# Earlier scaling for the wide score blocks of a gated linear recurrence, and one more weight step in front of them

## The chip, the cores and the metric

The kernel runs on one core of one Trainium2 chip. The metric is the device time of one execution in microseconds (us), as a median over runs; lower is better. The engines are called PE (TensorE matmul), PEld (its weight loads), DVE (VectorE), ACT (ScalarE), POOL (GpSimd) and SP (SyncE, which issues most transfers).

## The reference

One layer of a hybrid decoder on 1024 positions of width 1024, in float32. Two token mixers run beside each other, an RG-LRU and an HGRN2 recurrence with 8 heads of width 128; their outputs are merged by sigmoid gates, projected and added to the input. An MLP with a squared ReLU follows. The change lies in the HGRN2 part:

```python
def step(state, chunk):
    qc, kc, lfc, vc = chunk
    cum = jnp.cumsum(lfc, axis=2)
    o_inter = jnp.einsum('bhtk,bhkv->bhtv', qc * jnp.exp(cum), state)
    rel = cum[:, :, :, None, :] - cum[:, :, None, :, :]
    decay = jnp.where(causal[:, :, None], jnp.exp(jnp.minimum(rel, 0.0)), 0.0)
    scores = jnp.einsum('bhtsk,bhsk->bhts', qc[:, :, :, None, :] * decay, kc)
    o_intra = jnp.einsum('bhts,bhsv->bhtv', scores, vc)
    ...
    state = jnp.exp(last)[..., None] * state + jnp.einsum('bhsk,bhsv->bhkv', k_to_end, vc)
    return state, o_inter + o_intra
```

The kernel never takes logarithms: it multiplies keys and queries by products of forget gates over blocks of growing width (2, 8, 32, 64, 128 positions), so that each block of scores is a plain matrix product.

## The kernel before, in words

The sequence is worked in two parts of 512 positions (`c` = 0, 1), and in each part the heads go in four pairs (`p` = 0 to 3). So the code around the change runs eight times, once for each (c, p); these are called the eight pairs below, the first four with c = 0. After each part comes the output projection, and at the end the MLP, which the change doesn't touch.

A pair projects v, xa, q and f, then starts `hgrn`. While `hgrn` builds its operands on DVE, PE works on the projections g, mb, ga and ma of the same pair. They are a generator, `rest`, of 32 steps; a step is six products of 128x512 (`mm3` three times two, L123 to L125), and eight steps make one projection. `go(n)` runs n steps. The list `GO` says how many run before each part of `hgrn`: 17 steps before the narrow score blocks, GO[1] before the wide ones, then one before the transposes of the keys, one before the products that make the states, two before the output products, and the rest at the end. All products inside a pair are pinned: PE keeps the order in which the code issues them. DVE and ACT take the order that a scheduler gave them at build time.

The steps that matter, with the lines of the profile:

- narrow score blocks, L420: `pt1`, `pt2` (level 2) and `pt8` (level 8), 32 products of 128x48 each; DVE copies them under masks into `dd` (L410 and L431 for the own block, L439 six times for the levels), and POOL copies `dd` into `scT` (L515)
- scaling on DVE (`mul`, L410): first `kc` in place, then `qb` in place twice, then `kk` from `kc` and `qf` from `qb`; ACT copies the other halves of `kk` and `qf` (L528, L529)
- wide score blocks: 16 products from `kc` and `qb` (L538, block of 32) and 8 from `kk` and `qf` (L549, block of 64); ACT copies both into `scT` (L554, L555)
- `kk` and `qf` scaled once more by halves (L410), transposes of `kk` (`pk`, L576), ACT copies `kT` (L580), products `pkv` (L585), states `sn` on DVE (L594, L596), output products `po` (L610, L613), ACT squares and copies (L617, L623), the scaled output `on` on DVE (L410), transposes `poT` (L655)
- between these, weights of later projections are split into two parts: a cast on ACT (`wH`, L78) and a subtraction on DVE (`wL`, L79)

PSUM has eight banks under three tags: `pj` with four for the projections, `sc` and `hg` with two each, taken in turn. Before the change `pt1`, `pt2` and both wide blocks are under `sc`; `pt8`, `pk`, `pkv`, `po` and `poT` are under `hg`.

Of the kernel before, what the change touches and what calls it, by code (L numbers as in the profile page):

```python
# [18 lines left out]
P = 128  # L19
# [12 lines left out]
OUT_TILES = 8  # L32
QUADS = 16
LEVELS = (2, 8)
GO = (17, 4, 1, 1, 2)
OWN_BEFORE = 2


# [5 lines left out]
def trunk(ctx: ExitStack, tc: tile.TileContext, x, wts, mlp, pv, gains, mask_f, mask_u, out):  # L44
    nc = tc.nc
    V, A, G, PE = nc.vector, nc.scalar, nc.gpsimd, nc.tensor
# [13 lines left out]
    def bank(tag, name):  # L60
        return ps.tile([P, 512], F32, tag=tag, name=name, bufs={"pj": 4, "sc": 2, "hg": 2}[tag])
# [116 lines left out]
    def mt(tag, name, shape=(P, T), dt=F32, bufs=1):  # L178
        return m.tile(list(shape), dt, tag=tag, name=name, bufs=bufs)
# [111 lines left out]
    def run(steps, n=None):  # L291
        while n is None or n > 0:
            try:
                next(steps)
            except StopIteration as end:
                return end.value
            if n is not None:
                n -= 1
# [95 lines left out]
    def f_of(c, p, pp):  # L394
        ff = mt("f", f"f{c}{p}", (P, 2 * T))
        kk = mt("kk", f"kk{c}{p}", (P, 2 * T))
        for s in range(2):
            u = 2 * p + s
            f, k = ff[:, s * T : (s + 1) * T], kk[:, s * T : (s + 1) * T]
            A.activation(f, pp[s], AF.Sigmoid)  # L400
            A.activation(k, pp[s], AF.Sigmoid, scale=-1.0)
            V.tensor_scalar(f, f, omlb[:, u : u + 1], lb[:, u : u + 1], op0=ALU.mult, op1=ALU.add)
            V.tensor_scalar(k, k, omlb[:, u : u + 1], None, op0=ALU.mult)
        V.tensor_scalar(ff, ff, F_MIN, 1.0, op0=ALU.max, op1=ALU.min)
        return ff, kk

    def hgrn(c, p, q1, f, kk, v, go, scan):

        nm = f"{c}{p}"
        mul = lambda o, a, b: V.tensor_tensor(out=o, in0=a, in1=b, op=ALU.mult)  # L410
        dd = mt("dd", f"dd{nm}", (P, 8, 32))

        def blocks(k_, rhs, name, tag="sc"):

            pt = bank(tag, f"sc{name}_{nm}")[:, : 8 * 48].rearrange("p (n t) -> p n t", n=8)
            for n in range(8):
                for b in range(4):
                    k = 4 * n + b
                    pin(
                        PE.matmul(  # L420
                            pt[32 * b : 32 * b + 32, n, :], k_[:, 32 * k : 32 * k + 32], rhs(k), start=True, stop=True
                        )
                    )
            return pt

        def own_block(pt):
            pt = pt.rearrange("p n (a b) -> p n a b", b=3)
            d2 = dd.rearrange("p n (a b) -> p n a b", b=2)
            mf2 = mf.rearrange("p (a b) -> p a b", b=2).unsqueeze(1)
            mul(d2, pt[:, :, :, 0:2], mf2.to_broadcast([P, 8, 16, 2]))  # L430
            V.copy_predicated(dd[:, :, 1::2], mu[:, 0, :, 1::2], pt[:, :, :, 2])  # L431

        def level_blocks(li, cw, pt):
            pt = pt.rearrange("p n (a x) -> p (n a) x", x=6 * cw)
            dg = dd.rearrange("p n (a x) -> p (n a) x", x=4 * cw)
            for d, a in ((1, 0), (2, 3), (3, 5)):
                w = (4 - d) * cw
                m_ = mu[:, 3 * li + d, :, :].rearrange("p n (a x) -> p (n a) x", x=4 * cw)
                V.copy_predicated(dg[:, :, d * cw :], m_[:, :, d * cw :], pt[:, :, a * cw : a * cw + w])  # L439
# [4 lines left out]
        qa = mt("qa", f"qa{nm}", (P, 1792)).rearrange("p (a b c) -> p a b c", b=7, c=2)  # L444
# [13 lines left out]
        def take(n):  # L458
            nonlocal off
            off += n  # L460
            return seg[:, off - n : off]

        def sums(t4, g):
            after = take(3 * g).rearrange("p (a b) -> p a b", b=3)
            before = take(2 * g).rearrange("p (a b) -> p a b", b=2)
            mul(before[:, :, 0], t4[:, :, 0], t4[:, :, 1])
            mul(after[:, :, 1], t4[:, :, 2], t4[:, :, 3])
            G.tensor_scalar(after[:, :, 2], t4[:, :, 3], 1.0, 0.0, op0=ALU.mult, op1=ALU.add)  # L468
            mul(before[:, :, 1], before[:, :, 0], t4[:, :, 2])
            mul(after[:, :, 0], t4[:, :, 1], after[:, :, 1])  # L470
            return before, after

        def level_q(q4, t4, g, cw):
            mul(q4[:, :, 5, :], q4[:, :, 3, :], t4[:, :, 2:3].to_broadcast([P, g, cw]))
            mul(q4[:, :, 4:7:2, :], q4[:, :, 2:6:3, :], t4[:, :, 1:2].unsqueeze(3).to_broadcast([P, g, 2, cw]))

        c0, c1 = LEVELS
# [4 lines left out]
        kc = mt("kc", f"kc{nm}", (P, 2 * T))  # L482
# [14 lines left out]
        level_q(q4, t4, g1, c1)  # L497
        go(GO[0] - (OWN_BEFORE if c > 0 else 0))
        pt1 = blocks(kk, lambda k: q1[:, 16 * k : 16 * k + 16, :], "1")
        if c > 0:  # L500
            go(OWN_BEFORE)
        pt2 = blocks(kb, lambda k: qa[:, k * g0 // 32 : (k + 1) * g0 // 32, 1:7, :], str(c0))
        pt8 = blocks(kc, lambda k: q4[:, k * g1 // 32 : (k + 1) * g1 // 32, 1:7, :], str(c1), "hg")
        before, after = sums(t4, g1)
        own_block(pt1)
        level_blocks(0, c0, pt2)
        level_blocks(1, c1, pt8)
        mul(k4(kc, c1)[:, :, 0:3, :], k4(kc, c1)[:, :, 0:3, :], after.unsqueeze(3).to_broadcast([P, g1, 3, c1]))
        mul(q4[:, :, 1, :], q4[:, :, 1, :], t4[:, :, 0:1].to_broadcast([P, g1, c1]))
        mul(q4[:, :, 2:4, :], q4[:, :, 2:4, :], before.unsqueeze(3).to_broadcast([P, g1, 2, c1]))  # L510
        tc_ = take(g1)
        mul(tc_, before[:, :, 0], after[:, :, 1])
        qv = qb[:, :, 0:32]
        for b in range(4):
            G.tensor_scalar(  # L515
                scT[32 * b : 32 * b + 32, :, 32 * b : 32 * b + 32],
                dd[32 * b : 32 * b + 32, :, :],
                1.0,
                0.0,
                op0=ALU.mult,  # L520
                op1=ALU.add,
            )

        q8 = qv.rearrange("p (a e) c -> p a e c", e=2)
        pairs = lambda k: k.rearrange("p (a e c) -> p a e c", e=2, c=32)
        t8 = tc_.rearrange("p (a e) -> p a e", e=2)
        qf = mt("qa", f"qf{nm}", (P, 1792))[:, 0:1024]
        A.copy(pairs(kk)[:, :, 1, :], pairs(kc)[:, :, 1, :])  # L528
        A.copy(pairs(qf)[:, :, 0, :], q8[:, :, 0, :])  # L529
        mul(pairs(kk)[:, :, 0, :], pairs(kc)[:, :, 0, :], t8[:, :, 1:2].to_broadcast([P, 16, 32]))  # L530
        mul(pairs(qf)[:, :, 1, :], q8[:, :, 1, :], t8[:, :, 0:1].to_broadcast([P, 16, 32]))
        go(GO[1])
        pt = bank("sc", f"sc32_{nm}")[:, :256].rearrange("p (n t) -> p n t", n=8)
        for n in range(8):
            for b in (0, 2):
                k = 4 * n + b
# [34 lines left out]
        vn = lambda s, n: v[:, n, s * P : (s + 1) * P]  # L571
        go(GO[2])
        pk = [bank("hg", f"pk{c}{u}") for _, u in both]
# [4 lines left out]
        for s, u in both:  # L578
            kT.append(mt(("kT", "rr")[s], f"kT{c}{u}", (P, 4, P)))
            A.copy(kT[s][:, :nkv, :], pk[s][:, : nkv * P].rearrange("p (n k) -> p n k", n=nkv))  # L580
        go(GO[3])
        pkv = [bank("hg", f"pkv{c}{u}") for _, u in both]
# [5 lines left out]
        for s, u in both:  # L588
            sn = sn2[:, s]
            states.append([scar[:, u, :]] + [sn[:, n, :] for n in range(4)])  # L590
            for n in range(nkv):
# [3 lines left out]
                else:  # L595
# [7 lines left out]
                    )  # L603
        go(GO[4])
        po = [bank("hg", f"po{c}{u}") for _, u in both]
# [89 lines left out]
    for c in range(NC):  # L695
# [6 lines left out]
        for p in range(NPAIR):  # L702
            v = project_v(c, f"{c}{p}")
            px = project(c, f"xa{c}{p}")
            if c == 0 and p == 0:
                parameters()
                tc.keep_in_program_order(V.tensor_copy(mu, mu32.to_broadcast([P, 7, 8, 32])))
            xc3 = conv(c, p, px)
            pinned[0] = True
            q1 = q_of(c, p, project(c, f"q{c}{p}"))  # L710
            steps = project_steps(c, f"f{c}{p}")
            run(steps, 2)
            got = {}
            with tc.high_priority(300):
                rg = rg_lru(c, p, *xc3)
            f, kk = f_of(c, p, run(steps))
            rest = gates(c, p, got, ys)


            def scan():  # L720
                got["h"] = rg_scan(c, p, *rg)

            got["on"] = hgrn(c, p, q1, f, kk, v, lambda n: run(rest, n), scan)
            run(rest)
            pinned[0] = False
# [209 lines left out]
    for q in range(QUADS):  # L935
        n = q + 1 if q + 1 < QUADS else QUADS + QUADS - 2
# [79 lines left out]
    for kb in range(n_kb):  # L1016
        last = kb + 1 == n_kb
        qs = order[2 * kb : 2 * kb + 2]
        for half in range(2):
            pairs = (2 * half, 2 * half + 1)  # L1020
# [110 lines left out]
```

## Time and profile before

| | |
|---|---|
| median of 3 runs | 1605.46 us (1605.14, 1605.46, 1609.54) |
| profiled execution, its own time | 1608.64 us |
| its span, first to last instruction | 1606.8 us |
| busy share of PE, DVE, ACT | 97%, 75%, 47% |
| mean granted clock of PE | 0.995 of full |

Rows of the timeline have the start in us from the span's start, the duration in us, the engine, the line, the operation and its tiles, how many were merged into the row (`x32` for 16 products counts their weight loads too), and in brackets the idle time of the engine just before, with what ended it. Rows of the waits name who waited, for whom, and then the total in us, the number of times and the longest. Products overlap in PE, so their durations add up to more than the time that passes; the difference of two starts is the better measure.

### The profile page before, as it was taken

What the parts mean: (1) busy time and instruction counts of PE and PEld (TensorE: products, weight loads), DVE (VectorE), ACT (ScalarE), POOL (GpSimd) and SP (SyncE); (2) the same over time, 40 slices, a digit from 0 to 9 for tenths busy, and PEclk for the clock granted to TensorE, in tenths of its full rate; (3) what the DMA queues carried; (4) which work ended last, traced back from release to release, by engine and by line L of the source; (5) the groups of instructions that cost most, each with busy time, mean ns of one, the idle gap of its engine ahead of it and who ended that gap; (6) DMA issues with size and microseconds to landing.
All of it is one profiled execution on the core that took longest, in us unless ns stands there. A gap on an engine that the chain in (4) does not pass through costs nothing.

```text
span 1606.8 us, 23139 instructions
## 1 busy us (share of the span) xinstructions
PE 1562.4 (97%) x9240; PEld 1306.6 (81%) x9240; DVE 1200.3 (75%) x1703; ACT 748.8 (47%) x1186; POOL 92.7 (6%) x107
## 2 busy tenths in 40 slices
PE   7999999999999999999999997999999999999998
PEld 6888888788788888798888875888888878888886
DVE  5885865848853774956858788888888888888876
ACT  4643445345333544445435465766777731222113
POOL 0020010200200110100100100000000000000000
PEclk9999999999999999999999998999999999999999
DMA  6212212222243222222222362666666675666652
GB/s 239 93 66 92 93 66 101 83 80 92 80 168 134 92 79 80 93 79 96 76 92 92 120 209 103 251 239 253 254 236 249 233 266 227 254 251 255 257 206 105
DMA packets 57996, 246.51 MB, mean 153 GB/s; under 512 B 6688, under 2 KB 6816, under 8 KB 47136
## 3 DMA queue, kind: packets, MB, share of 16 engines
q1 hardware_dynamic: 56304, 239.27, 39.8%
q10 hardware_dynamic: 1584, 5.77, 1.0%
q8 instruction: 72, 1.18, 0.3%
q14 instruction: 36, 0.29, 0.1%
HBM read 185.24 MB, written 59.77 MB: 152 GB/s over the span
## 4 chain that ended last, share of the span: by engine, by line
PE 78%; DVE 15%; issue 2%; ACT 2%; DMA 1%; POOL 1%; DVEq 0%; POOLq 0%; ACTq 0%; SPq 0%
PE dX L123 3%; PE dX L124 3%; PE dX L125 3%; PE uX L123 3%; PE uX L125 3%; PE uX L124 3%; DVE wL L79 2%; PE pj_ma L125 2%; PE pj_ma L123 2%; PE pj_xa L123 2%; PE pj_xa L124 2%; PE pj_ma L124 2%; PE pv L123 2%; PE pv L124 2%; PE pj_f L123 2%
## 5 line engine op out<-in xcount | busy, mean ns | idle before, releaser
L79 DVE TENSOR_TENSOR wL<-raw,wH 128x1024 fp32r<-128x1024 f32 x160 | 195.4, 1221 | 132.3 <-ACT wH L78 130.6
L78 ACT CAST wH<-raw 128x1024 fp32r<-128x1024 f32 x160 | 167.6, 1047 | 131.9 <-PE po L124 27.3
L1043 DVE TENSOR_TENSOR acc<-acc,dX 128x512 f32<-128x512 f32 x128 | 85.0, 683 | 29.4 <-PE dX L125 29.0
L78 ACT CAST wA<-q 128x512 fp32r<-128x512 f32 x32 | 19.8, 622 | 132.6 <-PE dX L125 101.4
L468 POOL TENSOR_SCALAR seg<-seg 128x128 f32<-128x128 f32 (+1 forms) x16 | 31.6, 1974 | 443.9 <-DVE seg L410 443.9
L1043 DVE TENSOR_TENSOR acc<-acc,dY 128x512 f32<-128x512 f32 x64 | 43.5, 685 | 15.6 <-PE dY L125 14.5
L369 DVE RECIPROCAL rr<-rr 128x512 f32<-128x512 f32 x16 | 53.5, 3341 | 0.0
L903 ACT ACTIVATE b<-b 128x512 f32<-128x512 f32 x48 | 30.2, 630 | 37.4 <-DVE b L902 37.4
L364 DVE TENSOR_SCALAR rw<-rw 128x1024 f32<-128x1024 f32 x8 | 5.5, 694 | 43.7 <-ACT rw L360 43.7
L123 PE MATMUL pv<-wH,hT0H 128*128 128x256 f32 x128 | 37.2, 291 | 0.0
L124 PE MATMUL pv<-wL,hT0H 128*128 128x256 f32 x128 | 36.9, 288 | 0.0
L125 PE MATMUL pv<-wH,hT0L 128*128 128x256 f32 x128 | 36.8, 288 | 0.0
L123 PE MATMUL pv<-wH,hT1H 128*128 128x256 f32 x128 | 36.5, 285 | 0.0
L124 PE MATMUL pv<-wL,hT1H 128*128 128x256 f32 x128 | 36.2, 283 | 0.0
L125 PE MATMUL pv<-wH,hT1L 128*128 128x256 f32 x128 | 36.2, 283 | 0.0
L332 DVE SCALAR_TENSOR_TENSOR xc<-xp,pvt,xc 128x512 f32<-128x512 f32 x48 | 33.1, 745 | 0.0
L904 ACT ACTIVATE b<-b 128x512 f32<-128x512 f32 x48 | 30.0, 630 | 1.1
L79 DVE TENSOR_TENSOR wA<-q,wA 128x512 fp32r<-128x512 f32 x32 | 22.0, 687 | 10.1 <-ACT wA L78 9.8
L528 ACT COPY kk<-kc 128x512 f32<-128x512 f32 x8 | 5.0, 622 | 52.5 <-DVE kc L410 52.5
L515 POOL TENSOR_SCALAR scT<-dd 32x256 f32<-32x256 f32 x32 | 24.2, 756 | 82.2 <-DVE dd L439 80.7
L123 PE MATMUL pj_ga<-hT0H,wH 128*128 128x512 f32 x64 | 27.1, 424 | 0.0
L123 PE MATMUL pj_ga<-hT1H,wH 128*128 128x512 f32 x64 | 26.6, 416 | 0.0
(1860 smaller groups left out, 5231.1 us busy)
## 6 DMA issues: line engine op xcount, KB each, us to landing
raw<-wts_in SPq DMA_DIRECT2D x160, 512.0 KB, 3.4
q<-mlp_in SPq DMA_DIRECT2D x64, 512.0 KB, 4.0
x<-x_in SPq DMA_DIRECT2D x8, 512.0 KB, 5.8
acc<-x ACTq DMA_DIRECT2D x8, 512.0 KB, 5.3
y_out<-acc SPq DMA_DIRECT2D x16, 256.0 KB, 2.0
xs<-x_in SPq DMA_DIRECT2D x8, 256.0 KB, 3.4
x<-xs SPq DMA_DIRECT2D x8, 256.0 KB, 2.3
x2s<-x_in SPq DMA_DIRECT2D x4, 512.0 KB, 4.3
```

What stands on the lines that cost most here:

```text
L78: keep(A.copy(h, src))
L79: keep(V.tensor_tensor(out=lo, in0=src, in1=h.bitcast(F32), op=ALU.subtract))
L123: pin(PE.matmul(o, ah, bh, start=first, stop=False, **how))
L124: pin(PE.matmul(o, ah, bl, start=False, stop=False, **how))
L125: pin(PE.matmul(o, al, bh, start=False, stop=last, **how))
L332: V.scalar_tensor_tensor(xc[:, s, :], xp[:, j : j + T], pvt[:, PV_CW + 8 * j + u : PV_CW + 8 * j + u + 1], xc[:, s, :], op0=ALU.mult, op1= ...
L369: V.reciprocal(rec[:, s, :], rec[:, s, :])
L468: G.tensor_scalar(after[:, :, 2], t4[:, :, 3], 1.0, 0.0, op0=ALU.mult, op1=ALU.add)
L515: G.tensor_scalar(scT[32 * b : 32 * b + 32, :, 32 * b : 32 * b + 32], dd[32 * b : 32 * b + 32, :, :], 1.0, 0.0, op0=ALU.mult, op1=ALU.add,)
L903: A.activation(b[:, at, :], b[:, at, :], AF.Relu, scale=-1.0 if at == 2 else 1.0)
L904: A.activation(b[:, at, :], b[:, at, :], AF.Square)
L1043: V.tensor_tensor(out=dst, in0=dst, in1=banks[bk, pr], op=op)
```

## The change

Three things are done together in `hgrn`. The six `mul` that scale `kc`, `qb`, `kk` and `qf`, and the two ACT copies beside them, are written in front of the mask copies of the two levels (`level_blocks`) instead of between and behind them. The block of 32 takes its bank under `hg` instead of `sc`. And GO[1] is 5 instead of 4, so one more step of the projections stands in front of the wide blocks and one fewer behind the output products; all six kinds of products from the block of 32 to `po` come one step later in PE's order. No instruction is added or taken away.

```diff
-GO = (17, 4, 1, 1, 2)
+GO = (17, 5, 1, 1, 2)
...
-        own_block(pt1)
-        level_blocks(0, c0, pt2)
-        level_blocks(1, c1, pt8)
         mul(k4(kc, c1)[:, :, 0:3, :], k4(kc, c1)[:, :, 0:3, :], after.unsqueeze(3).to_broadcast([P, g1, 3, c1]))
         mul(q4[:, :, 1, :], q4[:, :, 1, :], t4[:, :, 0:1].to_broadcast([P, g1, c1]))
         mul(q4[:, :, 2:4, :], q4[:, :, 2:4, :], before.unsqueeze(3).to_broadcast([P, g1, 2, c1]))
+        own_block(pt1)
         tc_ = take(g1)
         mul(tc_, before[:, :, 0], after[:, :, 1])
         qv = qb[:, :, 0:32]
+        q8 = qv.rearrange("p (a e) c -> p a e c", e=2)
...
+        A.copy(pairs(kk)[:, :, 1, :], pairs(kc)[:, :, 1, :])
+        A.copy(pairs(qf)[:, :, 0, :], q8[:, :, 0, :])
+        mul(pairs(kk)[:, :, 0, :], pairs(kc)[:, :, 0, :], t8[:, :, 1:2].to_broadcast([P, 16, 32]))
+        mul(pairs(qf)[:, :, 1, :], q8[:, :, 1, :], t8[:, :, 0:1].to_broadcast([P, 16, 32]))
+        level_blocks(0, c0, pt2)
+        level_blocks(1, c1, pt8)
...
-        q8 = qv.rearrange("p (a e) c -> p a e c", e=2)
...
-        A.copy(pairs(kk)[:, :, 1, :], pairs(kc)[:, :, 1, :])
-        A.copy(pairs(qf)[:, :, 0, :], q8[:, :, 0, :])
-        mul(pairs(kk)[:, :, 0, :], pairs(kc)[:, :, 0, :], t8[:, :, 1:2].to_broadcast([P, 16, 32]))
-        mul(pairs(qf)[:, :, 1, :], q8[:, :, 1, :], t8[:, :, 0:1].to_broadcast([P, 16, 32]))
         go(GO[1])
-        pt = bank("sc", f"sc32_{nm}")[:, :256].rearrange("p (n t) -> p n t", n=8)
+        pt = bank("hg", f"sc32_{nm}")[:, :256].rearrange("p (n t) -> p n t", n=8)
```

What this does to the order of instructions is shown for the first pair (c = 0, p = 0). On PE, around the place where the wide blocks go now (`sc_00` are the two blocks, `pk` the transposed keys):

```order
 L124 MATMUL pj_ga_1_802<-hT0L_109,wH_769 128x512
 L125 MATMUL pj_ga_1_802<-hT0H_107,wL_770 128x512
-L576 MATMUL pk_1026<-ident,kk_631 128x128 x4
-L576 MATMUL pk_1027<-ident,kk_631 128x128 x4
+L538 MATMUL sc_00_976<-qb_650,kc_658 32x32 x16
+L549 MATMUL sc_00_993<-qf_925,kk_631 64x64 x8
 L123 MATMUL pj_ga_0_801<-hT0H_107,wH_769 128x512
```

The wide blocks stand where the transposes stood, and these in turn have moved to the place of `pkv`, one step later; `pkv` now follows the last product of ga.

On DVE, right behind the scaling of `kc` (`dd` rows are the mask copies):

```order
+L410 TENSOR_TENSOR qb_650<-qb_650,seg_643 128x32x8
+L410 TENSOR_TENSOR qb_650<-qb_650,seg_643 128x32x16
+L410 TENSOR_TENSOR kk_631<-kc_658,seg_643 128x16x32
+L410 TENSOR_TENSOR qf_925<-qb_650,seg_643 128x16x32
 L439 COPY_PREDICATED dd_641<-mu,sc_00_848 128x32x4
-L410 TENSOR_TENSOR qb_650<-qb_650,seg_643 128x32x8
 L439 COPY_PREDICATED dd_641<-mu,sc_00_848 128x32x2
-L410 TENSOR_TENSOR qb_650<-qb_650,seg_643 128x32x16
 L439 COPY_PREDICATED dd_641<-mu,sc_00_881 128x8x24
-L410 TENSOR_TENSOR kk_631<-kc_658,seg_643 128x16x32
 L439 COPY_PREDICATED dd_641<-mu,sc_00_881 128x8x16
-L410 TENSOR_TENSOR qf_935<-qb_650,seg_643 128x16x32
```

The four scalings that alternated with mask copies now stand in a row in front of five of the six copies.

On DVE, further down in the same pair, where the states `sn` are made:

```order
-L594 COPY sn_1056<-pkv_1046 128x128
-L596 TENSOR_SCALAR sn_1056<-sn_1056,seg_643,pkv_1046 128x128 x2
-L594 COPY sn_1056<-pkv_1047 128x128
-L596 TENSOR_SCALAR sn_1056<-sn_1056,seg_643,pkv_1046 128x128
-L596 TENSOR_SCALAR sn_1056<-sn_1056,seg_643,pkv_1047 128x128 x3
+L410 TENSOR_TENSOR qf_925<-qf_925,seg_643 128x8x64
 L79 TENSOR_TENSOR wL_1086<-raw_1083,wH_1085 128x1024
+L594 COPY sn_1062<-pkv_1052 128x128
+L594 COPY sn_1062<-pkv_1053 128x128
```

The subtraction for a later weight (`wL_1086`, for v of the next pair) stood behind the states and now stands in front of them. In the pairs with c = 1 it stands behind the first state.

More of the change, by code (lines that the diff above doesn't have):

```diff
@@ L513, in hgrn @@
         qv = qb[:, :, 0:32]
+        q8 = qv.rearrange("p (a e) c -> p a e c", e=2)
+        pairs = lambda k: k.rearrange("p (a e c) -> p a e c", e=2, c=32)
+        t8 = tc_.rearrange("p (a e) -> p a e", e=2)
+        qf = mt("qa", f"qf{nm}", (P, 1792))[:, 0:1024]
+        A.copy(pairs(kk)[:, :, 1, :], pairs(kc)[:, :, 1, :])
[4 more added lines that the diff above has]
+        level_blocks(1, c1, pt8)
         for b in range(4):
@@ L522, in hgrn @@
             )
-        q8 = qv.rearrange("p (a e) c -> p a e c", e=2)
-        pairs = lambda k: k.rearrange("p (a e c) -> p a e c", e=2, c=32)
-        t8 = tc_.rearrange("p (a e) -> p a e", e=2)
-        qf = mt("qa", f"qf{nm}", (P, 1792))[:, 0:1024]
-        A.copy(pairs(kk)[:, :, 1, :], pairs(kc)[:, :, 1, :])
-        A.copy(pairs(qf)[:, :, 0, :], q8[:, :, 0, :])
-        mul(pairs(kk)[:, :, 0, :], pairs(kc)[:, :, 0, :], t8[:, :, 1:2].to_broadcast([P, 16, 32]))
-        mul(pairs(qf)[:, :, 1, :], q8[:, :, 1, :], t8[:, :, 0:1].to_broadcast([P, 16, 32]))
         go(GO[1])
-        pt = bank("sc", f"sc32_{nm}")[:, :256].rearrange("p (n t) -> p n t", n=8)
+        pt = bank("hg", f"sc32_{nm}")[:, :256].rearrange("p (n t) -> p n t", n=8)
         for n in range(8):
```

## The prediction

> **What bounds the kernel now.** I read the page first, then PE's waits, then the timelines of PE and DVE around the wide blocks of all eight pairs.
>
> ```profile
> PE 1562.4 (97%) x9240; PEld 1306.6 (81%) x9240; DVE 1200.3 (75%) x1703; ACT 748.8 (47%) x1186; POOL 92.7 (6%) x107
> PE sc L549 <- DVE dd L439: 6.3, 7, 1.0
> PE sc L538 <- DVE qb L410: 3.6, 4, 1.6
> PE sc L549 <- ACT wH L78: 1.0, 1, 1.0
> ```
>
> PE is busy for 97% of the span, so time is to be had only where PE stands still. Inside the pairs that is at two lines: in front of the block of 64 (L549) in all eight pairs, 6.3 + 1.0 us, and in front of the block of 32 (L538) in four, 3.6 us. Together 10.9 us. The names in these rows need care; PE's timeline in the first pair and in the fifth (c = 1) says when the waits end:
>
> ```profile
> 98.42 0.39 PE L124 MATMUL pj_ga<-hT0L,wH 128*128 128x512 f32 x1
> 98.65 0.39 PE L125 MATMUL pj_ga<-hT0H,wL 128*128 128x512 f32 x1
> 99.73 0.70 PE L538 MATMUL sc<-qb,kc 128*32 128x32 f32 x32 [0.69 <-DVE qb L410]
> 101.39 1.12 PE L549 MATMUL sc<-qf,kk 128*64 128x64 f32 x16 [0.97 <-DVE dd L439]
> 102.44 0.50 PE L123 MATMUL pj_ga<-hT0H,wH 128*128 128x512 f32 x1
> ...
> 573.80 0.39 PE L125 MATMUL pj_ga<-hT1H,wL 128*128 128x512 f32 x1
> 574.14 0.70 PE L538 MATMUL sc<-qb,kc 128*32 128x32 f32 x32
> 575.81 1.12 PE L549 MATMUL sc<-qf,kk 128*64 128x64 f32 x16 [0.97 <-DVE dd L439]
> 576.86 0.50 PE L123 MATMUL pj_ga<-hT1H,wH 128*128 128x512 f32 x1
> ```
>
> From the last ga product to the next one 3.79 us pass in the first pair and 3.06 in the fifth. DVE in the first pair shows for what:
>
> ```profile
> 97.38 0.93 DVE L410 TENSOR_TENSOR kc<-kc,seg 128x768 f32<-128x768 f32 x1
> 98.23 0.29 DVE L439 COPY_PREDICATED dd<-mu,sc 128x128 f32<-128x128 uint8 x1
> 98.43 0.42 DVE L410 TENSOR_TENSOR qb<-qb,seg 128x256 f32<-128x256 f32 x1
> 98.76 0.28 DVE L439 COPY_PREDICATED dd<-mu,sc 128x64 f32<-128x64 uint8 x1
> 98.89 0.69 DVE L410 TENSOR_TENSOR qb<-qb,seg 128x512 f32<-128x512 f32 x1
> 99.50 0.36 DVE L439 COPY_PREDICATED dd<-mu,sc 128x192 f32<-128x192 uint8 x1
> 99.76 0.69 DVE L410 TENSOR_TENSOR kk<-kc,seg 128x512 f32<-128x512 f32 x1
> 100.36 0.30 DVE L439 COPY_PREDICATED dd<-mu,sc 128x128 f32<-128x128 uint8 x1
> 100.56 0.69 DVE L410 TENSOR_TENSOR qf<-qb,seg 128x512 f32<-128x512 f32 x1
> 101.16 0.22 DVE L439 COPY_PREDICATED dd<-mu,sc 128x64 f32<-128x64 uint8 x1
> 101.30 1.22 DVE L79 TENSOR_TENSOR wL<-raw,wH 128x1024 fp32r<-128x1024 f32 x1
> 102.55 0.77 DVE L410 TENSOR_TENSOR kk<-kk,seg 128x512 f32<-128x512 f32 x1
> ```
>
> The second scaling of `qb` ends at 99.58 and L538 starts at 99.73; `qf` ends at 101.25 and L549 starts at 101.39, 0.14 us later, although the table blames a mask copy: the last mask copy starts inside that gap and is what the table met. So both waits are for scaling on DVE, and four mask copies stand in the way.
>
> **Part 1: scaling in front of the mask copies.** Start to start, `kc` takes 0.85 us, the two `qb` 0.33 and 0.61, `kk` 0.60; `qf` takes 0.69 to its end. In a row from 97.38: `qb` at 98.23 and 98.56, `kk` 99.17, `qf` 99.77 to 100.46. `qf` is ready 0.79 us earlier. This alone would not free L549, which stands 0.97 us.
>
> **Part 2: one more step in front.** Six products at 0.23 us (98.42 to 98.65) are 1.38 us of work that PE has to do anyhow, so the move itself costs nothing. In the first pair L538 could start at 98.65 + 1.38 + 0.34 (573.80 to 574.14, a start without a wait) = 100.37, after `qb` is ready. L549 follows 0.5 to 0.7 us later (0.70 is L538's whole row), at about 100.95; `qf` is ready at 100.46 + 0.14 = 100.60. Margin 0.35 us. In the fifth pair the idle time before L538 is already nil and `qf` ends 0.79 us earlier too, so the margin is over a microsecond. Both waits go in seven pairs. The bank of the block of 32 is priced at nothing: its bank under `hg` was last read for the previous pair's `poT`; the block of 64 now gets the bank that `pt1` had, which DVE left before the scaling began.
>
> The fourth pair is later on DVE, since a norm of the next part stands in front:
>
> ```profile
> 417.56 0.43 DVE L439 COPY_PREDICATED dd<-mu,sc 128x192 f32<-128x192 uint8 x1
> 418.21 0.39 PE L125 MATMUL pj_ga<-hT0H,wL 128*128 128x512 f32 x1
> ```
>
> There the new order puts `kc` in the place of that first copy, so `qf` ends at 417.56 + 0.85 + 0.33 + 0.61 + 0.60 + 0.69 = 420.64, ready 420.78; L549 could start at 418.21 + 1.38 + 0.34 + 0.6 = 420.53. A wait of 0.25 us stays.
>
> **Part 3: what is late next.** These rows of the first pair are the followers:
>
> ```profile
> 103.96 1.04 PE L576 MATMUL pk<-ident,kk 128*128 128x128 f32 x8
> 106.22 1.95 PE L585 MATMUL pkv<-v,kT 128*128 128x128 f32 x16
> 107.31 0.29 DVE L594 COPY sn<-pkv 128x128 f32<-128x128 f32 x1 [3.19 <-PE pkv L585]
> 109.15 0.39 PE L125 MATMUL pj_ga<-hT0H,wL 128*128 128x512 f32 x1
> 110.53 1.22 DVE L79 TENSOR_TENSOR wL<-raw,wH 128x1024 fp32r<-128x1024 f32 x1 [0.68 <-ACT wH L78]
> 110.75 0.61 PE L610 MATMUL po<-v,scT 128*128 128x128 f32 x4
> 119.15 1.23 DVE L410 TENSOR_TENSOR on<-on,hrs 128x1024 f32<-128x1024 f32 x1 [1.77 <-POOL hrs L626]
> 123.45 1.03 PE L655 MATMUL poT<-ident,on 128*128 128x128 f32 x8
> ```
>
> *`pk` behind the half scaling of `kk`.* That scaling waits for L549 to have read `kk`, and on DVE for the mask copies and a `wL`, whose sum is unchanged: it starts at 102.55 as before and ends at 103.32, ready 103.46. `pk` would come at 100.95 + 1.05 (101.39 to 102.44) + 1.52 (102.44 to 103.96) = 103.52. It just fits; in the fourth pair, where all six copies (1.2 us together) follow `qf`, it does not: the half scaling ends at 420.55 + 1.2 + 1.2 + 0.7 = 423.65, ready 423.8, and `pk` would come at 420.78 + 1.05 + 1.52 = 423.35. With the 0.25 above, 0.7 us are given back.
>
> *States behind `wL`.* That `wL` (110.53) waits for a cast into a buffer which ga's last product frees; it started 1.38 us behind that product (109.15). Now ga's last product stands right in front of `pkv`, 0.23 us, so `wL` starts about 1.2 us behind `pkv` and ends 2.4 behind; the first state, which started 1.09 behind (106.22 to 107.31), is ready at 2.4 + 0.3 = 2.7. `po` comes 4.53 us behind `pkv` (106.22 to 110.75), and its first product that reads a state about 4.7 behind; the next ones take the states slower than DVE makes them. Margin 2.0 us, nothing lost.
>
> *`poT` behind `on`.* `on` ends at 120.38, `poT` starts at 123.45: 3.07 us, of which one step of 1.38 goes. 1.7 us are left.
>
> **The clock.** In the third pair the waits did more:
>
> ```profile
> 310.70:314.10 3.40, 1.70 (x46) 1.36 (x45) 3.40 (x9) 2.52 (x5) 0.56 (x1) 1.00 0.00 0
> 314.10:317.50 3.40, 3.40 (x14) 2.60 (x13) 1.90 (x3) 0.58 (x1) 2.67 (x4) 0.51 0.49 157
> ```
>
> Columns: the stretch, its length, PE, PEld, DVE, ACT and POOL busy, the granted clock. After 3.4 us in which PE was busy for 1.70, the next 3.4 us ran at 0.51 of the clock: 3.4 x 0.49 = 1.7 us of work lost at most; I take 1.5, since PE filled only part of it with full-width products. With the waits gone I expect the spell gone. The Trainium skill ("TensorE: Matmul & The Clock Gate", "What's actually happening") states that the rate falls to a half after at least one idle window of about 3.4 us, and that the windows run freely. The length agrees with the row, the condition does not: here a window that was busy for half of its time was followed by the low rate. By that rule the spell is not these waits' doing and would stay.
>
> **The sum.** Removed: 10.9 us of idle time. A product that follows without a wait also starts before the one in front has ended, where idle time counts from that end: no gain from that at the low end, at most 0.2 us (about the length of one small product) at eight places and less at four, 1.7 us, at the high end; these rows are near neither, I take 0.8. Given back: 0.7. That is 11.0, bounds 9.5 to 12.6. With the clock 12.5. Against the profiled execution: 1608.64 - 12.5 = 1596.1. That execution is 3.2 us over the median of 1605.46, about two such spells; if the median run had none at this place, 1605.46 - 11.0 = 1594.5. I forecast 1595.0, between the two, with 1592 to 1598 as this case's own range.
>
> **The rivals.**
>
> *The spell stays*, because something other than the waits sets it off. For it: one execution can't show that the gap caused it, and other pairs with similar waits had none. Against: it begins right behind a stretch that was busy for 1.70 of 3.40 us. Time: 1608.64 - 11.0 = 1597.6. Chance 0.15. The rule of the Trainium skill told above would make it so.
>
> *A new wait at `pk`.* The margin there is 0.06 us in the first pair, and the half scaling can't start before DVE has done five mask copies and `wL`. If it comes 0.6 us late in each pair, 4.8 us go: 1595.0 + 4.8 = 1599.8. Against: with c = 1 the margin is larger. Chance 0.14.
>
> *The change doesn't remove the wait*, because L549 waits for the last mask copy as the table says. That copy would still end at about 101.38, ready at 101.52, against 100.95 in the pairs with c = 0: 4 x 0.57 = 2.3 us less, 1597.3; or, with a release that the rows don't show, all 7.3 us of L549 stay and only L538's 3.6 go, 1605.46 - 3.6 = 1601.9. Against: the 0.14 us between `qf` and L549. Chance 0.06, mostly the second.
>
> *Slower: the states come too late for `po`.* `wL` now stands in front of the states on DVE, and waits for a cast on ACT, which waits for a weight buffer. If that buffer came free only four steps later (4 x 1.38 = 5.5 us), the first state would be there 2.7 + 5.5 = 8.2 us behind `pkv` and `po` stand for 8.2 - 4.7 = 3.5 us in each pair: 8 x 3.5 = 28, or 1595.0 + 28 = 1623. It decides from 2.0 us of delay on; from 4.5 us on it costs 8 x 2.5 = 20 us and the kernel is slower than before by more than 4.8. Against: before, this `wL` ran at 110.53, within two steps of ga's end, so the buffer is free by then. Chance 0.09.
>
> **How the numbers follow.** The main case has 0.56. A measurement can tell 0.3%, 4.8 us, from no change: faster is below 1600.6, slower above 1610.3. Faster: 0.56 + 0.15 + 0.09 of the new wait's 0.14 + 0.02 of the unremoved one's 0.06 = 0.82. Same: 0.05 + 0.04 = 0.09. Slower 0.09. The range goes from 1591.5 (1605.46 less the high bound of 12.6 and less 1.5, if the median run had one spell here) to 1601.5, which takes in the spell that stays and most of the new wait; the slower case and half of the unremoved wait are left out.
>
> **What would show it.** In the profile after, the waits of L538 and L549 are gone but for a few tenths in the fourth pair; from the last ga product to the next across the wide blocks about 2 us pass in every pair; `qf` is scaled right behind `kk`; `wL` runs before the states and PE does not stand at `po` or `poT`; the third pair has a granted clock of 1.00. The forecast is wrong if PE stands in front of `pk` or `po`, or if a half-rate spell comes up elsewhere.

## The result, and the profile after

The changed kernel takes 1596.66 us (median of 5 runs, 1596.34 to 1597.73); the kernel before takes 1605.46 us (1603.75 to 1609.54). The ratio is 0.9943, 95% interval 0.9929 to 0.9958. That is 8.8 us less where 10.5 were forecast. The profiled execution of the changed kernel took 1596.66 us, its span is 1594.8 us.

The page's first row, and the two rows of PE's waits that belong to the pairs (who waited, for whom, total us, times, longest):

```profile
PE 1560.4 (98%) x9240; PEld 1304.7 (82%) x9240; DVE 1202.2 (75%) x1703; ACT 748.7 (47%) x1186; POOL 88.2 (6%) x107
PE pk L576 <- DVE kk L410: 1.1, 2, 0.8
PE sc L549 <- DVE qf L410: 0.2, 1, 0.2
```

Of the 10.9 us in front of the wide blocks 0.2 are left. A row has come that wasn't there before: PE waits at `pk`. PE's timeline in the first pair:

```profile
99.92 0.39 PE L125 MATMUL pj_ga<-hT0H,wL 128*128 128x512 f32 x1
100.24 0.70 PE L538 MATMUL sc<-qb,kc 128*32 128x32 f32 x32
100.87 1.15 PE L549 MATMUL sc<-qf,kk 128*64 128x64 f32 x16
101.94 0.50 PE L123 MATMUL pj_ga<-hT0H,wH 128*128 128x512 f32 x1
...
103.21 0.39 PE L125 MATMUL pj_ga<-hT0H,wL 128*128 128x512 f32 x1
103.73 1.09 PE L576 MATMUL pk<-ident,kk 128*128 128x128 f32 x8
```

From the last ga product to the next across the wide blocks, called the stretch below, 2.02 us pass, where it was 3.79. All pairs show 2.02 us but the fourth, with 2.29. From the last of the step's products to `pk` 0.52 us pass, though `pk` needs about 0.23: with c = 1, 1.50 us lie between the first ga product behind the wide blocks and `pk`; here it is 1.79, and in the second to fourth pair 1.95, 1.80 and 2.41. Together PE stands there for 1.95 us. The short ones are only partly in the waits row, which counts from the end of the product in front.

DVE in the same pair says why:

```profile
97.14 0.93 DVE L410 TENSOR_TENSOR kc<-kc,seg 128x768 f32<-128x768 f32 x1
97.99 1.02 DVE L410 TENSOR_TENSOR qb<-qb,seg 128x256 f32<-128x256 f32 x2
98.92 0.68 DVE L410 TENSOR_TENSOR kk<-kc,seg 128x512 f32<-128x512 f32 x1
99.53 0.68 DVE L410 TENSOR_TENSOR qf<-qb,seg 128x512 f32<-128x512 f32 x1
100.13 1.62 DVE L439 COPY_PREDICATED dd<-mu,sc 128x128 f32<-128x128 uint8 x5
101.65 1.22 DVE L79 TENSOR_TENSOR wL<-raw,wH 128x1024 fp32r<-128x1024 f32 x1
102.79 0.88 DVE L410 TENSOR_TENSOR kk<-kk,seg 128x512 f32<-128x512 f32 x1
```

The scalings take what was forecast. The five mask copies behind them take 1.52 us from the first to `wL`; spread between the scalings the same five took 0.20 + 0.13 + 0.26 + 0.20 + 0.14 = 0.93. So the half scaling of `kk` ends at 103.67 and PE starts `pk` at 103.73; in the other three pairs with c = 0 `pk` starts 0.05 to 0.06 us behind that end too.

### The profile page after: what moved, and what is told of

Read it like the earlier page. It is cut to its first block, busy times and chain, and to the rows that moved or that the text cites. A ratio compares the mean times of both kernels' runs of the same rounds, so it can differ in the third digit from the quotient of the medians.

```text
span 1594.8 us, 23146 instructions
## 1 busy us (share of the span) xinstructions
PE 1560.4 (98%) x9240; PEld 1304.7 (82%) x9240; DVE 1202.2 (75%) x1703; ACT 748.7 (47%) x1186; POOL 88.2 (6%) x107
## 4 chain that ended last, share of the span: by engine, by line
PE 67%; DVE 4%; DMA 1%; issue 1%; ACT 1%; POOL 0%; DVEq 0%; POOLq 0%; SPq 0%
PE dX L123 3%; PE dX L124 3%; PE dX L125 3%; PE uX L123 3%; PE uX L125 3%; PE uX L124 3%; PE dY L123 2%; PE dY L125 2%; PE dY L124 2%; PE uY L125 2%; PE uY L124 2%; PE uY L123 2%; PE po L124 2%; PE po L123 2%; PE po L125 2%; PE pj_ma L125 1%
## 5 line engine op out<-in xcount | busy, mean ns | idle before, releaser
L468 POOL TENSOR_SCALAR seg<-seg 128x128 f32<-128x128 f32 (+1 forms) x16 | 25.1, 1568 | 450.1 <-DVE seg L410 450.1
```

## Experiments

For each kernel the place of the last `poT` product, which ends the pairs, is the cleanest measure of what the pairs take, since the MLP behind it varies by itself (see the last section). In the changed kernel the row of that line ends with 903.3; the second trace of the kernel before (first experiment) has 912.2, in this order:

```profile
L655 PE MATMUL poT<-ident,on x64: 270/272/273, 121.9 to 903.3; 128*128 128x128 f32 x64
```

```profile
L655 PE MATMUL poT<-ident,on x64: 271/272/273, 123.5 to 912.2; 128*128 128x128 f32 x64
```

| kernel | GO[1] | scaling first | bank of the block of 32 | median us | ratio to before, 95% interval | last `poT`, us |
|---|---|---|---|---|---|---|
| before, a second trace | 4 | no | sc | 1604.56 (one run) | | 912.2 |
| changed, again | 5 | yes | hg | 1597.30 | 0.9944 (0.9930 to 0.9958) | 903.2 |
| step alone | 5 | no | sc | 1595.23 | 0.9932 (0.9919 to 0.9944) | 903.1 |
| scaling alone | 4 | yes | sc | 1607.35 | 1.0004 (0.9995 to 1.0012) | 912.7 |
| old bank | 5 | yes | sc | 1597.05 | 0.9939 (0.9925 to 0.9952) | 903.5 |
| two steps | 6 | yes | hg | 1595.33 | 0.9932 (0.9919 to 0.9945) | 901.9 |
| two steps alone | 6 | no | sc | 1595.00 | 0.9929 (0.9916 to 0.9941) | 902.2 |
| one step less | 3 | no | sc | 1626.05 | 1.0125 (1.0109 to 1.0142) | 932.8 |

**The kernel before, a second time.** No edit.

> The kernel before, unchanged, for a second trace of it. Theory (PE's waits set the half-rate spell off, and the window in which the clock judges PE runs freely): the waits at the wide blocks are the same within 0.2 us a pair, but the half-rate spell of 3.4 us at 314 us need not be there again; it may be gone or stand at another pair, and the time differs from the 1608.64 us of the first profiled execution by about 1.5 us for each spell more or fewer. Rival (the spell belongs to that place of the program): it stands at 314 us again.

The waits are the same (6.3, 1.0 and 3.5 us), and there is no half-rate spell (3.4 us at half the granted clock) in any pair. The profiled execution is 4.1 us shorter than the first, with two such spells fewer, the one at 314 us and one at 1000 us, early in the MLP. The windows of 3.4 us lie elsewhere against the program this time; they are counted back from the spell that this trace has at 967.5 us, in steps of 3.413, the length of a single spell. Columns: stretch, length, PE, PEld, DVE, ACT and POOL busy, granted clock, DMA share, GB/s:

```profile
312.10:315.50 3.40, 2.51 (x43) 2.18 (x41) 3.37 (x7) 2.38 (x5) 1.89 (x2) 1.00 0.02 5
417.90:421.30 3.40, 1.83 (x49) 1.71 (x49) 3.36 (x7) 2.19 (x4) 0.00 (x0) 1.00 0.24 92
421.30:424.70 3.40, 3.40 (x19) 2.92 (x20) 1.52 (x3) 1.66 (x3) 2.24 (x4) 1.00 0.51 152
```

The third pair's gap now lies across two windows, and the emptiest one, in the fourth pair, has PE busy for 1.83 of 3.40 us and is followed by the full rate. The rival falls: the same program passes the place without a spell.

**The step alone.**

```diff
-GO = (17, 4, 1, 1, 2)
+GO = (17, 5, 1, 1, 2)
```

> The extra step alone: GO[1] is 5, the scaling stays between the mask copies and the block of 32 under its old tag. Theory (PE is given 1.38 us more before the wide blocks, which covers nearly all of the wait): the block of 32 waits nowhere but in the fourth pair; the block of 64 waits about 0.5 us in the first three pairs, 1.0 in the fourth, not at all in the last four; pk doesn't wait, since PE comes there later. 8.5 to 9.5 us less than before, about 1597 us, within 1 us of the changed kernel. Rival (the order on DVE carries the gain): about 1601 us.

```profile
101.36 1.12 PE L549 MATMUL sc<-qf,kk 128*64 128x64 f32 x16 [0.41 <-DVE dd L439]
102.41 0.50 PE L123 MATMUL pj_ga<-hT0H,wH 128*128 128x512 f32 x1
```

The block of 64 still waits 0.41 us in the first pair, a little less in the next two, 0.8 in the fourth, where the block of 32 waits 0.3 as well, and nowhere in the last four; `pk` never waits. The pairs end at 903.1, as in the changed kernel. So on PE the theory holds: one step carries the whole gain of the pairs, and what the earlier scaling adds at the wide blocks (2.0 us over the four pairs with c = 0) it gives back at `pk` (1.95 us). The median missed: it is 11.7 us under that of the kernel before on this chip (1606.88), where 8.5 to 9.5 were expected, and 1.4 us under the changed kernel's. In the profiled executions that difference lies behind the pairs, where 689.8 us follow here and 691.5 in the changed kernel.

**The scaling alone.**

```diff
 GO = (17, 4, 1, 1, 2)
...
+        mul(pairs(qf)[:, :, 1, :], q8[:, :, 1, :], t8[:, :, 0:1].to_broadcast([P, 16, 32]))
+        level_blocks(0, c0, pt2)
+        level_blocks(1, c1, pt8)
...
         pt = bank("sc", f"sc32_{nm}")[:, :256].rearrange("p (n t) -> p n t", n=8)
```

> The scaling in front of the mask copies alone: GO[1] is 4 and the block of 32 has its old tag. Theory: qf is ready 0.8 us earlier in all eight pairs, so each stretch across the wide blocks is 0.8 us shorter (1.1 in the fourth pair), 6.6 us; the transposes of the keys then come before the half scaling of kk in the pairs with c = 0 and give back 0.3 us each: 5.4 us less than before, about 1600 us. Rival (the order on DVE carries the gain): about 1597 us.

Both lines missed: nothing is gained. PE, and then DVE, in the first pair:

```profile
100.90 1.12 PE L549 MATMUL sc<-qf,kk 128*64 128x64 f32 x16 [1.03 <-DVE dd L439]
103.73 0.44 PE L576 MATMUL pk<-ident,kk 128*128 128x128 f32 x2
```

```profile
99.53 0.69 DVE L410 TENSOR_TENSOR qf<-qb,seg 128x512 f32<-128x512 f32 x1
100.14 1.61 DVE L439 COPY_PREDICATED dd<-mu,sc 128x128 f32<-128x128 uint8 x5
101.66 1.22 DVE L79 TENSOR_TENSOR wL<-raw,wH 128x1024 fp32r<-128x1024 f32 x1
```

`qf` ends at 100.22, but the block of 64 starts at 100.90. With the block of 32 under `sc` it has the bank of the level-2 scores, and the two copies that read them now follow `qf`, to about 100.75. So the stretches shrink by 2.0 us in all, 25.8 against 27.8, and not by 6.6; and `pk` comes 0.29 us late in seven pairs, which takes the 2.0 us back. The new bank without the step was not run. In the first pair it could not have brought `pk` forward: DVE works without a gap from `qf` to the end of the half scaling (103.68), and `pk` starts 0.05 us behind that.

**The old bank.**

```diff
-        pt = bank("hg", f"sc32_{nm}")[:, :256].rearrange("p (n t) -> p n t", n=8)
+        pt = bank("sc", f"sc32_{nm}")[:, :256].rearrange("p (n t) -> p n t", n=8)
```

> The changed kernel with the block of 32 under its old tag, so that the block of 64 gets the bank of the level-2 scores, which DVE reads after the scaling now. Theory (banks are priced at nothing while the mask copies end before PE comes): the level-2 copies end 0.35 us behind qf, which only the fourth pair feels: 0 to 0.6 us more than the changed kernel. Rival (the bank is what frees the block of 64): it waits for the mask copies in all eight pairs, 0.5 us or more each, 4 us or more.

```profile
416.41 1.11 PE L549 MATMUL sc<-qf,kk 128*64 128x64 f32 x16 [1.25 <-ACT scT L554]
```

```profile
415.18 1.08 DVE L439 COPY_PREDICATED dd<-mu,sc 128x192 f32<-128x192 uint8 x3
```

With the step in front, the bank matters in the fourth pair most: there the block of 64 waits until the three level-2 copies have ended (416.26, and 0.15 us later it starts; the copy on ACT that the table names reads the block of 32), a microsecond longer than with the new bank. `pk` doesn't wait in return. In the second and third pair the stretch is 0.2 us longer (2.24 and 2.22). The pairs end 0.2 us later. The theory holds.

**Two steps, with and without the scaling first, and the changed kernel beside them.** `GO = (17, 6, 1, 1, 2)` in the changed kernel and in the kernel before.

> The changed kernel, unchanged, beside the next two on the same chip. Theory (the five mask copies in a row take 0.6 us longer on DVE than spread between the scalings, so that the half scaling of kk and with it pk come late in the pairs with c = 0): the step alone, 1595.2 us on another chip, stays ahead of it by 0.5 to 2 us. Rival (the difference lies between chips): it comes out at 1595 us or below.

> The changed kernel with a second extra step, GO[1] is 6. Theory (what is left are the waits at pk in the first four pairs, 1.95 us, and 0.27 us at the block of 64 in the fourth): both go, 2.2 us less than the changed kernel, about 1594.5 us, and no wait at poT, where 2.4 us were left and a step is 1.4. Rival (the shorter way from po to poT becomes the bound): PE stands at poT and the time stays or rises.

> The kernel before with two extra steps, GO[1] is 6, the scaling left between the mask copies. Theory (the steps alone carry the gain): no wait at the wide blocks or at pk in any pair, 2.0 us from ga product to ga product across the wide blocks, the same time as the changed kernel with two extra steps within 1 us, about 1593.5 us. Rival (the order on DVE is needed): more than 2 us slower than that.

The changed kernel's 1597.30 us are 2.1 above the step alone, so the rival of two different chips falls. But the theory's reason, the wait at `pk`, doesn't explain them: the pairs end at 903.2 here and at 903.1 with the step alone. The difference lies behind the pairs, as it did above.

With two steps the wide blocks and `pk` have no wait left, in either order on DVE: 2.02 us across the wide blocks and 1.50 from there to `pk` in all eight pairs, with and without the scaling first. The pairs end 1.0 to 1.4 us earlier than in the changed kernel, less than the 2.2 expected; which other gaps took the rest is open. PE doesn't stand at `poT`. By time, 1595.33 and 1595.00 us are below the changed kernel's 1597.30 on the same chip, but the intervals of the ratios overlap. As a version, the kernel before with GO[1] at 5 or 6 is as good as the changed one or better by a microsecond or two, with one number changed.

**Mask copies into two tiles.** In the changed kernel, the copies of level 8 go into a second tile, `de`, in turn with those of level 2. POOL clears that tile first, and nothing reads it, so the level-8 scores are missing from the output.

```diff
-        level_blocks(0, c0, pt2)
-        level_blocks(1, c1, pt8)
+        de = mt("rr", f"de{nm}", (P, 4, P)).rearrange("p a b -> p (a b)")[:, 0:256]
+        G.memset(de, 0.0)
+        dd2[0] = de.rearrange("p (n a) -> p n a", n=8)
+        level_blocks(0, c0, pt2, ((1, 0), (2, 3)))
+        level_blocks(1, c1, pt8, ((1, 0),))
+        level_blocks(0, c0, pt2, ((3, 5),))
+        level_blocks(1, c1, pt8, ((2, 3), (3, 5)))
```

> The changed kernel, with the mask copies of level 8 written into a tile of their own, in turn with those of level 2; the level-8 scores are then missing from the output. Theory (a copy waits for the end of the copy in front because it writes the same tile): three of the five copies now follow one that writes another tile, and start 0.13 to 0.27 us behind it as they did behind a scaling, instead of 0.32 to 0.41; from the first copy to wL 1.1 us instead of 1.53, and pk comes 0.3 us less late in the first three pairs. Rival (masked copies behind each other are slow as such): 1.5 us as before.

```profile
100.25 0.29 DVE L440 COPY_PREDICATED dd<-mu,sc 128x128 f32<-128x128 uint8 x1
100.44 0.37 DVE L440 COPY_PREDICATED de<-mu,sc 128x192 f32<-128x192 uint8 x1
100.71 0.29 DVE L440 COPY_PREDICATED dd<-mu,sc 128x64 f32<-128x64 uint8 x1
100.85 0.56 DVE L440 COPY_PREDICATED de<-mu,sc 128x128 f32<-128x128 uint8 x2
101.31 1.31 DVE L79 TENSOR_TENSOR wL<-raw,wH 128x1024 fp32r<-128x1024 f32 x1
```

From the first copy to `wL` 1.06 us pass instead of 1.52. Behind a copy into the other tile the next one starts after 0.19, 0.27 and 0.14 us; the last two write the same tile, and there the second starts when the first has ended. So it is not masked copies as such: a copy that writes the tile of the copy in front waits for its end. Nor is it that both read one bank: in the changed kernel the third of the five reads another bank than the second, and still starts 0.03 us behind its end. `pk` comes 1.62 us behind the first ga product instead of 1.79, 0.17 less late where 0.3 was expected. Over the four pairs with c = 0 PE stands at `pk` for 0.8 us where it was 1.95, and the pairs end at 901.8.

**One step less.**

```diff
-GO = (17, 4, 1, 1, 2)
+GO = (17, 3, 1, 1, 2)
```

> The kernel before with one step less in front of the wide blocks, GO[1] is 3: each wait there grows by the 1.38 us of a step, 11 us in all, so about 1618 us by the waits alone. Theory (a window of 3.4 us in which PE is busy for less than about half sets a half-rate spell off, as in the third pair of the first profile): windows that lie over the longer stretches, 5.2 us in the pairs with c = 0 and 4.4 with c = 1, now fall below half in most of the first four pairs, and the trace shows three or more spells among the eight pairs, at 1.5 us each: 1622 to 1628 us. Rival (a spell needs a window with no work at all, as the Trainium skill's page on TensorE and the clock gate has it): no spell among the pairs, 1616 to 1620 us.

```profile
97.80:101.20 3.40, 0.70 (x32) 0.62 (x32) 3.40 (x9) 2.09 (x3) 0.00 (x0) 1.00 0.00 0
101.20:104.60 3.40, 3.17 (x19) 2.89 (x20) 2.55 (x5) 1.30 (x4) 2.77 (x4) 0.50 0.31 93
316.30:319.70 3.40, 1.36 (x43) 1.31 (x44) 3.40 (x9) 2.56 (x5) 0.52 (x1) 1.00 0.00 0
319.70:323.10 3.40, 3.40 (x14) 2.60 (x13) 2.19 (x3) 0.58 (x1) 2.60 (x4) 0.50 0.46 151
906.80:910.20 3.40, 2.03 (x49) 1.91 (x50) 3.37 (x8) 2.37 (x5) 1.18 (x1) 1.00 0.02 5
910.20:913.60 3.40, 3.40 (x20) 2.83 (x20) 1.40 (x2) 1.27 (x3) 1.94 (x4) 1.00 0.44 154
```

The kernel is 20.4 us slower than the kernel before on the same chip (1605.62). The waits at the wide blocks grow by 11 us (21.9 against 10.8); the other 9.4 fit the half-rate spells, at about 1.5 us each. The trace has six of them among the eight pairs, each right behind a window in which PE was busy for 1.36 us or less; the two pairs without one had no window below 2.01. The rival's 1616 to 1620 us are missed by 6.

## Why the prediction was right, point by point

- *What bounds the kernel.* Right: the waits at the wide blocks were to be had, and the block of 64 waited for `qf` and not for the mask copy that the table names: in all eight pairs of the kernel before it starts 0.14 to 0.15 us behind the end of `qf`. One step more, with the order on DVE left as it was, takes the 6.3 + 1.0 us at the block of 64 down to 1.6.
- *Part 1, `qf` 0.79 us earlier.* Right as a duration (`kc` to the end of `qf` 3.07 us, forecast 3.08), but worth nothing to the whole. I had written that it alone would not free the block of 64; alone, with the old bank, it gave 1.0004. The sum counts waits and not what each part does to them, so it could come out although this part adds nothing: the step alone shortens the stretches by 9.4 us (27.8 to 18.4) and costs nothing at `pk`, the whole change by 11.4 less the 2.0 at `pk`, again 9.4.
- *Part 2, one more step at no cost.* Right: the starts of both blocks were within 0.13 us of the working (100.24 for 100.37, 100.87 for 100.95). The wait left in the fourth pair was 0.23 us, forecast 0.25. The bank priced at nothing: right for the whole change, 0.2 us; beside the scaling alone the old bank holds the block of 64 back by 0.5 us in seven pairs and 1.0 in the fourth, which I had not seen.
- *Part 3, `pk` behind the half scaling.* This is the step that failed, by the forecast's own sign of being wrong: PE stands in front of `pk`. I wrote that the mask copies' and `wL`'s sum on DVE is unchanged; it grew by 0.6 us, because copies in a row into one tile wait for each other. The margin of 0.06 us became a wait in all four pairs with c = 0: 1.95 us where 0.45 were counted. The rival of a new wait at `pk` was thus true for half of the pairs, at 0.5 us each. These 1.5 us are nearly all that the sum of the pairs lacks: 9.4 us measured (below) where 11.0 were forecast.
- *States behind `wL`, `poT` behind `on`.* Right. `wL` starts 1.13 us behind `pkv` (forecast 1.2) and the first state follows it at 2.27; `po` keeps its 4.53 us. From the end of `on` to `poT` 2.4 us are left, more than the 1.7 forecast. The rows of DVE and PE:

```profile
107.18 1.22 DVE L79 TENSOR_TENSOR wL<-raw,wH 128x1024 fp32r<-128x1024 f32 x1 [2.71 <-ACT wH L78]
108.32 0.48 DVE L594 COPY sn<-pkv 128x128 f32<-128x128 f32 x2
118.29 1.23 DVE L410 TENSOR_TENSOR on<-on,hrs 128x1024 f32<-128x1024 f32 x1 [1.77 <-POOL hrs L626]
```

```profile
106.05 1.61 PE L585 MATMUL pkv<-v,kT 128*128 128x128 f32 x13
110.58 0.61 PE L610 MATMUL po<-v,scT 128*128 128x128 f32 x4
121.92 0.49 PE L655 MATMUL poT<-ident,on 128*128 128x128 f32 x3
```

- *The clock.* The cause was right: in the pairs a window in which PE is busy for half of the time or less sets the spell off, and the changed kernel's pairs have neither. But the 1.5 us belonged to the one profiled execution; whether the median one had such a spell no run shows. That the forecast went 0.5 us from 1594.5 towards that execution brought it nearer to the result, and was luck.
- *The sum.* Between the profiled executions 1608.64 - 1596.66 = 12.0 us went, forecast 12.5. Between the traces without a spell in the pairs, the stretches lost 27.8 - 16.4 = 11.4 us and `pk` gave back 2.0; the pairs end 8.9 us earlier. About half a microsecond is not assigned. The 0.8 us taken for products that start before the one in front has ended came out: 11.4 less the 10.6 us of waits that went. The low bound of 9.5 does not follow from the terms given, which make it 10.9 - 0.7 = 10.2; the 9.4 measured lie under both, by what `pk` took.

## What to carry to other kernels

When an engine waits for a chain on another, first ask whether independent work can be moved in front of the waiting instruction: one step of products moved ahead was worth the whole gain, at no cost, while shortening the chain by 0.8 us, alone or beside the step, was worth nothing to the pairs here. When instructions are regrouped, their sum is not what it was: five short copies into one tile cost 0.9 us spread between other work and 1.5 in a row. And where a trace of one execution shows a half-rate spell, price it apart, since the next execution may not have it.

## What the runs showed of the hardware

Around the wide blocks of the pairs, the granted clock fell to a half for the next 3.4 us when PE had been busy for no more than about half of a window of 3.4 us. In all eleven traces the windows there that were followed by a spell had 1.71 us of work or less (0.70, 1.36, 1.70 in the rows shown), those with 1.82 and more had none. The rule of the Trainium skill ("TensorE: Matmul & The Clock Gate", "What's actually happening") asks for an idle window; in the pairs PE was never idle for a whole one, so these runs show the low rate under a milder condition. That the windows run freely agrees with the two traces of the same kernel, one with a spell and one without.

PE's busy time alone does not give the limit, as two windows behind the pairs show, the first with two steps alone, the second in the kernel before:

```profile
919.34:922.75 3.41, 1.57 (x12) 1.45 (x12) 2.83 (x3) 1.39 (x3) 0.45 (x1) 1.00 0.29 101
922.75:926.16 3.41, 3.41 (x17) 2.81 (x16) 2.36 (x3) 2.60 (x5) 0.00 (x0) 1.00 0.75 274
```

```profile
996.81:1000.22 3.41, 1.80 (x7) 1.18 (x8) 1.85 (x3) 1.50 (x3) 0.00 (x0) 1.00 0.00 0
1000.22:1003.63 3.41, 3.41 (x10) 2.65 (x9) 0.67 (x2) 0.00 (x0) 0.00 (x0) 0.50 0.63 229
```

After 1.57 us of work the full rate stayed, and after 1.80 it fell. What the clock goes by is left open.

The spells also make the times scatter: the norms in front of the MLP have one in every trace, and a second one, behind a wait of 2 us for a weight cast early in the MLP (`uX` for `ws30H`), comes and goes from trace to trace. In the four traces without it 689.8 to 691.4 us follow the last `poT`, in the seven with it 691.5 to 692.7. Whether that explains all of the spread of the kernel before (1604 to 1609 us) is left open.
